# A hybrid decoder step on one core: the sample's cross attention takes its cache unsplit, and four instead of six couples of up-projection tiles are begun early

## The chip, the core and the metric

The kernel runs on one core of one Trainium2 chip. The core has five engines with instruction queues of their own: TensorE (PE; its weight loads are shown apart as PEld), VectorE (DVE), ScalarE (ACT), GpSimd (POOL) and SyncE (SP), which here issues nearly all transfers. Each queue is worked off in order, and engines wait for one another through semaphores. The metric is the device time of one launch in microseconds, lower being better. The kernel before was run three times: median 2275.94 us, 2272.01 to 2283.53.

## The reference, cut to what matters

A prompt of 1024 rows and 8 samples of 8 rows go through one layer that shares all weights. The four token mixers come first; the two parts that the change touches are the last two steps:

```python
x = _ln(ALPHA * x + mix, lp['ln1_g'], lp['ln1_b'])
qm = (x @ lp['w_mq']).reshape(n, L, X_HEADS, X_HD)
s = jnp.einsum('nqhe,nkhe->nhqk', qm, mem_k, preferred_element_type=jnp.float32) * (X_HD ** -0.5)
pr = jax.nn.softmax(s, axis=-1)
att = jnp.einsum('nhqk,nkhe->nqhe', pr.astype(mem_v.dtype), mem_v).reshape(n, L, D_MODEL) @ lp['w_mo']
x = _ln(ALPHA * x + att, lp['ln2_g'], lp['ln2_b'])
ff = jnp.square(jax.nn.relu(x @ lp['w_up'])) @ lp['w_down']
x = _ln(ALPHA * x + ff, lp['ln3_g'], lp['ln3_b'])
```

There are 4 heads of 256 and 256 memory tokens. For the samples `mem_k` and `mem_v` are caches of their own (`cache_mem_k`, `cache_mem_v`: 8 samples x 256 x 4 x 256 each, 16.8 MB together), so every sample multiplies with another matrix and has only 8 query rows for it. The feed forward is 1024 x 4096 and back.

## The kernel before, in words

All is float32. A large product is made from matmuls on float32r operands: an operand is split into `hi`, its rounded copy (made by ACT), and `lo`, the remainder (subtracted by DVE), and `hi*hi + hi*lo + lo*hi` are summed in PSUM. `split_w` (L85 to L108) does this to a 128x1024 weight tile: one 512 KB load into a `raw` buffer by SP, one cast (L100), one subtraction (L106).

**Cross attention** (`rest`, from L1589). For the prompt, sixteen steps over eight tiles of 128 rows and two head pairs `hp` make the scores: `scores` is 24 matmuls of 512 columns into `sc` (L129), then a softmax on ACT and DVE, and later four transposes (`ptr`, L1505) turn the probabilities. After each step's softmax, `next(sample)` takes some steps of the generator `sample_x`, which holds the samples' attention, so its instructions stand between those of the prompt. In `sample_x` the query rows are first made with `w_mq` (`acc`) and turned (`qtr`). A part is four samples and one head pair. For each part `own` lays out a stationary operand with zeros for other samples' queries, and each of the four samples' key tiles goes through `split_w` and eight matmuls of 256 columns with 64 stationary columns (`sps`, L1553). The same is done with the value tiles into `ops` (L1578). `spread` (L1566) multiplies each part's result with a constant `sel` to turn it (`otr`). That is 32 tiles, 32 casts, 32 subtractions and 256 matmuls of this kind. The loads take `raw` buffers from a ring of four (`wraw2` and `wraw`, two each). After the last step the folded output weights (`fold`) and `w_mo` are loaded through the two buffers of `wraw` (`out_proj`, from L1372).

**Feed forward** (`feed`, from L1664). The up projection is done by a two-by-two scheme of the Strassen kind over sixteen couples `p` of column tiles: seven products of blocks for four, on pieces of `x` called `11`, `21`, `22`, `t1` to `t4`. Class `Hat` makes the pieces from the rows turned on PE: `first` makes `11` and `21`, `second` makes `22` and `t2` tile by tile, `rest` makes `t3`, `t1` and `t4`. A product is 24 matmuls of 272 columns (L117). `begin(p)` does a couple's two products with `11` and `21` ahead of the loop, while `Hat.second` still works on the rest: couples 0 and 1 keep the results (`vr`), the others write them to DRAM (`vd`) from the pool `vs`, and `recall` brings them back inside the loop. The piece `t4` takes the memory of the pool `vs`, so it is made after the last write to `vd` has gone out. Then the loop over the couples makes the other products in the order `t2`, `t3`, `t1`, `t4`, `22`, and for a couple that was not begun early also `11` and `21`. The weight sums `s1` to `s4` that these need are made by `first_sums` on POOL (`sw`, L1779 and L1780) and by `prep` on DVE (L1792, L1794); `split` (L1686, L1687) makes the operands `wo`, up to three ahead. Each couple's results are combined on POOL (`sh`, L1925 to L1928) and written to DRAM (`hs`); `w_down` blocks are summed on DVE and written as `wt`. All of these transfers are issued by SP in the order of the code, tied by `behind` (L1695).

The order of instructions in each queue is settled when the program is built, by a scheduler that moves independent work up or down.

Of the kernel before, what the change touches and what calls it, by code (L numbers as in the profile page):

```python
# [8 lines left out]
F32 = mybir.dt.float32  # L9
F32R = mybir.dt.float32r  # L10
# [30 lines left out]

LOADS, SPLITS, TAIL, OX = 4, 2, 6, 12

EARLY_PAIRS = 6

MORE = [(0, i) for i in range(1, 8)] + [(1, 0)]
UNITS = dict(first=8, pre=1, blk=1, u1=1, chain=1, smp=1, norm=1, d0=3, d1=1, z=1)
# [2 lines left out]
class Kern:  # L50
# [1457 lines left out]
    def sample_x(self, x1, out):  # L1508

        nc, I, pm = self.nc, self.I, self.pm
        sel = pm.tile([64, 32], F32, name="sel")
        nc.sync.dma_start(sel, I["sel"])
        z = pm.tile([128, 512], F32, name="zs")
        qs = pm.tile([128, 8, 64], F32, name="qs")
        row = lambda name: pm.tile([128, 512], F32, name=name, tag="row", bufs=2)

        def own(src, name):

            t = pm.tile([128, 4, 4, 64], F32R, name=name, tag="own", bufs=2)
            nc.vector.memset(t.rearrange("p a s x -> p (a s x)").bitcast(F32), 0.0)
            t4 = t.rearrange("p (a b) s x -> p a b s x", b=2)
            for s4 in range(4):
                v, c = src(s4), 8 * s4
                nc.scalar.copy(t4[:, :, :, s4, c:c + 8], v)
                nc.vector.tensor_sub(t4[:, :, :, s4, 32 + c:40 + c], v, t4[:, :, :, s4, c:c + 8].bitcast(F32))
# [16 lines left out]
        parts = [(s2, hp) for s2 in range(2) for hp in range(2)]  # L1544
        for s2, hp in parts:
            qz = own(lambda s4: qs[:, 4 * hp:4 * hp + 4, 32 * s2 + 8 * s4:32 * s2 + 8 * s4 + 8].rearrange("p (a b) q -> p a b q", b=2), "qz")
            ps = self.wk_ps("sps", "acc")
            for s4 in range(4):
                w = self.split_w(I["cmk"][4 * s2 + s4, hp])
                for h in range(2):  # L1550
                    for ct in range(2):
                        for i in range(2):
                            nc.tensor.matmul(ps[0:64, h * 256:h * 256 + 256], qz[:, 2 * h + ct, s4, :], w[i][:, (2 * h + ct) * 256:(2 * h + ct) * 256 + 256],  # L1553
                                             start=s4 == h == ct == i == 0, stop=s4 == 3 and h == ct == i == 1)
                yield
            r, lo = slice(64 * s2 + 32 * hp, 64 * s2 + 32 * hp + 32), row("slo")
            nc.scalar.copy(lo[r], ps[32:64])
            nc.vector.tensor_add(z[r], lo[r], ps[0:32])
        pT = pm.tile([128, 4, 128], F32, name="pTs")
        nc.scalar.copy(pT, self.keys_first(self.softmax(z, "ps")))  # L1560
        pT = pT.rearrange("p (h k) (s a t) -> p k h s a t", k=2, s=2, a=2)
        def spread(s2, hp, o):

            tr = self.wk_ps("otr")[:, 0:128].rearrange("p (k t) -> p k t", t=32)
            for k in range(4):
                nc.tensor.matmul(tr[:, k, :], o[0:64, k * 128:k * 128 + 128], sel, start=True, stop=True)  # L1566
            nc.scalar.copy(out[:, 4 * hp:4 * hp + 4, 32 * s2:32 * s2 + 32], tr)

        last = None
        for s2, hp in parts:  # L1570
            pz = own(lambda s4: pT[:, :, :, s2, hp, 8 * s4:8 * s4 + 8], "pz")
            ps = self.wk_ps("ops", "acc")
            for s4 in range(4):
                w = self.split_w(I["cmv"][4 * s2 + s4, hp])
                for kb in range(2):
                    for h in range(2):
                        for i in range(2):
                            nc.tensor.matmul(ps[0:64, h * 256:h * 256 + 256], pz[:, 2 * kb + h, s4, :], w[i][:, (2 * kb + h) * 256:(2 * kb + h) * 256 + 256],  # L1578
                                             start=s4 == kb == h == i == 0, stop=s4 == 3 and kb == h == i == 1)
                if s4 == 1 and last:  # L1580
                    spread(*last)
                yield
            o = row("so")
            nc.scalar.copy(o[0:64], ps[0:64])
            last = s2, hp, o
        yield
        spread(*last)

# [75 lines left out]
    def feed(self, hat, y, s_xb, s_y, w3, w4, wb):  # L1664
# [89 lines left out]
        hat.second(y, 5, self.gp)  # L1754
        begin(1)
        hat.second(y, 6, self.gp)
        begin(2)
        hat.second(y, 7, self.gp)
        begin(3)
        begin(4)  # L1760
        begin(5)
        fetch(0)
        fetch(1)
        hat.rest("t3")
        hat.rest("t1")
        s_t4.close()
        hat.room(s_up.enter_context(self.pool("xh4", side="right")), ("t4",))
        hat.rest("t4")
        s_y.close()
        self.mmp, self.mmi = ring4 + [self.psw] * 4, -1  # L1770
        up = s_up.enter_context(self.pool("uh"))
# [34 lines left out]
        todo, ops = operands(), []  # L1806

        def nxt():
            while len(ops) < (3 if not st["wide"] else 4):
# [377 lines left out]
def _consts():  # L2187
# [31 lines left out]
    return {"sel": np.tile(np.eye(32, dtype=f), (2, 1)), "cmask": cm, "amask": am, "tmask": tm, "smask": np.tile(sm, (128, 1)), "teye": te.reshape(128, 8, 32), "ident": np.eye(128, dtype=f)}  # L2219


def _prep(a):
# [95 lines left out]
```

## Time and profile before

| what | value |
|---|---|
| median of three runs | 2275.94 us |
| the profiled execution | 2281.47 us, its span 2279.7 us |
| mean granted TensorE clock | 0.977 of full |
| PE, PEld busy | 95%, 86% |
| DVE, ACT, POOL busy | 60%, 43%, 19% |
| chain that ended last | PE 71%, DVE 10%, DMA 9%, issue 4%, ACT 3%, POOL 2% |

The busy shares are means over stages that differ, and the chain tells which work the end waited for. A matmul's duration in a row includes the time to run empty; the distance between starts is what a stream of them costs. Rows name output and inputs by the program's names, `x16` counts instructions, and what stands in brackets is the idle time of that engine before the row and what ended it.

### The profile page before, as it was taken

The page shows a single profiled execution, that of the slowest core. Times are in us where ns is not written, and L with a number is a line of the kernel's source. Part 1 is how long each engine was busy: PE and PEld are TensorE (multiplying, and loading weights), DVE is VectorE, ACT ScalarE, POOL GpSimd, SP SyncE. Part 2 cuts the span into 40 slices and gives each one's busy share as a digit, 9 for nine tenths or more (in the row PEclk, how much of TensorE's full clock was granted, in tenths as well). Part 3 has the DMA queues.
Part 4 walks back from the last instruction along what each step waited for, and adds up shares of the span by engine and source line. Part 5 has one row for each costly group of instructions (what it writes and reads, how often), then busy time and mean ns, then how long its engine had stood idle before and what let it go on. Part 6 is the DMA issues. An engine that isn't in the chain of part 4 may idle for free.

```text
span 2279.7 us, 36377 instructions
## 1 busy us (share of the span) xinstructions
PE 2175.1 (95%) x13702; PEld 1949.2 (86%) x13702; DVE 1374.5 (60%) x2748; ACT 978.7 (43%) x1888; POOL 425.7 (19%) x484
## 2 busy tenths in 40 slices
PE   8998999999999999999999999998789999999997
PEld 8987777898989888998998888778789999788886
DVE  3356767755665764343333877586667776655558
ACT  4333433145555655444231566335334444543432
POOL 0111111012311200123220500000445444100100
PEclk9998989999999999999999999999899999999999
DMA  5322333135444435555324355624487767975534
GB/s 191 103 75 61 99 90 98 38 129 186 152 132 130 130 114 171 162 173 162 102 64 149 120 190 167 221 102 141 162 292 261 248 238 239 325 240 182 178 118 171
DMA packets 186071, 359.41 MB, mean 158 GB/s; under 512 B 36312, under 2 KB 92776, under 8 KB 185896
## 3 DMA queue, kind: packets, MB, share of 16 engines
q1 hardware_dynamic: 175448, 321.52, 43.2%
q0 software_dynamic: 10448, 35.57, 4.6%
q8 instruction: 108, 1.77, 0.3%
q14 instruction: 67, 0.55, 0.1%
HBM read 252.18 MB, written 104.84 MB: 157 GB/s over the span
## 4 chain that ended last, share of the span: by engine, by line
PE 71%; DVE 10%; DMA 9%; issue 4%; ACT 3%; POOL 2%; SPq 1%; DVEq 0%; ACTq 0%; POOLq 0%
PE mm L117 21%; PE m L117 12%; PE dn L1989 11%; PE mm L129 8%; PE sc L129 3%; PE pp L117 3%; PE ds L1994 1%; DVE tpr L1013 1%; DVE wlo L106 1%; DMA vp<-in_vpages,pt 1%; ACT whi L100 1%; DMA Li<-Ld 1%; PE wtp L502 1%; DVE Ti L1014 1%; PE gr L965 1%
## 5 line engine op out<-in xcount | busy, mean ns | idle before, releaser
L117 PE MATMUL mm<-ah,whi 128*128 128x384 f32 (+1 forms) x1176 | 395.7, 336 | 8.4 <-ACT ah L277 4.9
L117 PE MATMUL mm<-al,whi 128*128 128x384 f32 (+1 forms) x1176 | 392.5, 334 | 0.6 <-DVE al L278 0.6
L117 PE MATMUL mm<-ah,wlo 128*128 128x384 f32 (+1 forms) x1176 | 391.7, 333 | 0.6 <-DVE wlo L106 0.6
L1989 PE MATMUL dn<-dop 128*128 128x512 f32 x1344 | 318.8, 391 | 3.7 <-ACT dop L1686 3.5
L1989 PEld LDWEIGHTS dn<-dop 128*128 128x128 f32 x1344 | 251.7, 188 | 60.6 <-ACT dop L1686 5.2
L106 DVE TENSOR_TENSOR wlo<-wraw,whi 128x1024 fp32r<-128x1024 f32 (+2 forms) x177 | 196.1, 1117 | 174.1 <-ACT whi L100 172.6
L100 ACT CAST whi<-wraw 128x1024 fp32r<-128x1024 f32 (+1 forms) x162 | 165.8, 1032 | 258.0 <-PE mm L117 101.6
L117 PEld LDWEIGHTS mm<-ah,whi 128*128 128x128 f32 x1176 | 224.4, 191 | 18.0 <-ACT ah L277 5.5
L117 PEld LDWEIGHTS mm<-al,whi 128*128 128x128 f32 x1176 | 224.1, 191 | 7.0 <-issue 3.5
L117 PEld LDWEIGHTS mm<-ah,wlo 128*128 128x128 f32 x1176 | 224.1, 191 | 4.3 <-issue 1.9
L1687 DVE TENSOR_TENSOR dop<-wraw,dop 128x512 fp32r<-128x512 f32 x224 | 151.3, 712 | 118.2 <-ACT dop L1686 117.6
L117 PE MATMUL m<-xht,wo 128*128 128x272 f32 x1024 | 202.7, 293 | 16.8 <-ACT wo L1686 10.5
L1686 ACT CAST dop<-wraw 128x512 fp32r<-128x512 f32 x224 | 131.2, 619 | 167.8 <-PE dn L1989 117.3
L117 PEld LDWEIGHTS m<-xht,wo 128*128 128x128 f32 x1024 | 165.8, 192 | 17.7 <-ACT wo L1686 10.7
L129 PE MATMUL mm<-wlo,ah 128*128 128x512 f32 (+1 forms) x488 | 170.1, 351 | 2.7 <-DVE wlo L106 2.7
L129 PE MATMUL mm<-whi,ah 128*128 128x512 f32 (+1 forms) x488 | 170.5, 351 | 0.8 <-ACT stA L300 0.5
L117 PE MATMUL m<-xh,wo 128*128 128x272 f32 x768 | 153.6, 293 | 6.1 <-DVE r L1901 6.1
L129 PE MATMUL mm<-whi,al 128*128 128x512 f32 (+1 forms) x448 | 156.5, 349 | 0.0
L117 PE MATMUL m<-xlt,wo 128*128 128x272 f32 x512 | 149.5, 292 | 0.0
L117 PEld LDWEIGHTS m<-xh,wo 128*128 128x128 f32 x768 | 124.7, 192 | 6.7 <-ACT wo L1686 2.6
L117 PE MATMUL m<-xl,wo 128*128 128x272 f32 x384 | 111.9, 292 | 0.0
L129 PEld LDWEIGHTS mm<-wlo,ah 128*128 128x128 f32 x488 | 93.9, 193 | 16.7 <-DVE wlo L106 3.6
(510 smaller groups left out, 4313.1 us busy)
## 6 DMA issues: line engine op xcount, KB each, us to landing
wraw<-hs SPq DMA_DIRECT2D x112, 256.0 KB
wraw<-in_w_up SPq DMA_DIRECT2D x38, 512.0 KB
wraw<-in_w_gate SPq DMA_DIRECT2D x32, 512.0 KB
dw<-in_w_down SPq DMA_DIRECT2D x32, 512.0 KB
hs<-sh SPq DMA_DIRECT2D x64, 256.0 KB
wt<-dw SPq DMA_DIRECT2D x32, 512.0 KB
wraw<-wt SPq DMA_DIRECT2D x64, 256.0 KB
wraw<-in_w_down SPq DMA_DIRECT2D x48, 256.0 KB
```

Of the source, the lines that this page charges most:

```text
L100: nc.scalar.copy(hi[:, c], raw[:, c])
L106: nc.vector.tensor_sub(lo[:, c], raw[:, c], hi[:, c].bitcast(F32))
L117: nc.tensor.matmul(ps[:, :n], a, b, start=first and i == 0, stop=last and i == len(steps) - 1, skip_group_check=not first)
L129: nc.tensor.matmul(ps[:, :n], a, b, start=i == 0, stop=i == len(steps) - 1)
L502: self.nc.tensor.transpose(ps[:b.shape[-1], j * 128:j * 128 + 128], b, self.ident)
L965: nc.tensor.matmul(g[hh][:nb, j, :nb], p[HR[hh], pr, cs], q[HR[hh], pr, cs], start=True, stop=True)
L1013: nc.vector.tensor_mul(tv, Ti[:, 0:h, 0:t + 1], Li[:, 0:t + 1, t:t + 1].rearrange("p s o -> p o s").to_broadcast([128, h, t + 1]))
L1014: nc.vector.tensor_reduce(Ti[:, 0:h, t:t + 1], tv, axis=AX.X, op=ALU.add)
L1686: nc.scalar.copy(o[:, 0], src)
L1687: nc.vector.tensor_sub(o[:, 1], src, o[:, 0].bitcast(F32))
L1989: nc.tensor.matmul(ps[j], hs[:, a, c], w[:, b], start=first and k == 0, stop=last and k == 2, skip_group_check=n >= 16 and steps[n][0] in ...
L1994: nc.tensor.matmul(sp, rows[p][:, smp[i]].rearrange("p a n -> p (a n)"), ops[n][1][:, b], start=i != 2 and p == 0 and b == 0, stop=p == 15 ...
```

## The change

Two edits are made in one step. In `sample_x`, `split_w` is gone. `products` loads two samples' tiles at a time into the same `raw` buffers (now called `kvraw`) and multiplies them as they are, in float32: eight matmuls of 256 columns for two samples, each with 32 stationary columns, and the result of head `h` and sample `s` goes to its own 32 PSUM rows (`r = 64 * h + 32 * s`). A group of eight has four such row blocks in turn, twice. There are 16 groups, so 128 matmuls. A `raw` buffer is now held until its matmuls have read it. `spread` turns the result with two transposes for a head pair, twice instead of four times four matmuls. In `feed`, couples 4 and 5 are no longer begun early; `fetch(0)` stands earlier, and couple 0's weight sums are made by DVE in place, and its operands split, before `t3`, `t1` and `t4`, instead of by `first_sums(0)` after them.

```diff
-EARLY_PAIRS = 6
+EARLY_PAIRS = 4
...
-            t = pm.tile([128, 4, 4, 64], F32R, name=name, tag="own", bufs=2)
+            t = pm.tile([128, 4, 2, 4, 32], F32, name=name, tag="own", bufs=2)
...
+        def raw(src):
+            self.wi += 1
+            t = self.raws[self.wi % len(self.raws)].tile([128, 1024], F32, name="kvraw", tag="raw")
+            nc.sync.dma_start(t, src)
+            return t
+
+        def products(ps, o, name, hp, col, first, last):
+
+            for j in range(4):
+                w = []
+                for a in range(2):
+                    w.append(raw(I[name][2 * j + a, hp]))
+                    if a:
+                        for i in range(2):
+                            for h in range(2):
+                                c, st = col(h, i)
+                                for s in range(2):
+                                    r = 64 * h + 32 * s
+                                    nc.tensor.matmul(ps[r:r + 32, o:o + 256], st[:, s, j, :], w[s][:, 256 * c:256 * c + 256],
+                                                     start=first and j == i == 0, stop=last and j == 3 and i == 1)
+                    yield
...
-            for s4 in range(4):
-                w = self.split_w(I["cmk"][4 * s2 + s4, hp])
...
-                            nc.tensor.matmul(ps[0:64, h * 256:h * 256 + 256], qz[:, 2 * h + ct, s4, :], w[i][:, (2 * h + ct) * 256:(2 * h + ct) * 256 + 256],
...
+        ps = self.wk_ps("sps", "acc")
+        for hp in range(2):
+            qz = own(lambda j: qs[:, 4 * hp:4 * hp + 4, 16 * j:16 * j + 16].rearrange("p k (s q) -> p k s q", q=8), "qz")
+            yield from products(ps, 256 * hp, "cmk", hp, lambda h, ct: (2 * h + ct, qz[:, 2 * h + ct]), hp == 0, hp == 1)
...
-                nc.tensor.matmul(tr[:, k, :], o[0:64, k * 128:k * 128 + 128], sel, start=True, stop=True)
+                nc.tensor.transpose(tr[:, 128 * k:128 * k + 128], o[:, 128 * k:128 * k + 128], self.ident)
...
         hat.second(y, 6, self.gp)
+        fetch(0)
         begin(2)
         hat.second(y, 7, self.gp)
         begin(3)
-        begin(4)
-        begin(5)
-        fetch(0)
+
+        a11, a12, a21, a22 = blocks(0)
+        x0 = hat.pool.tile([128, 512], F32, name="x0", tag="ex8", bufs=1)
+        nc.vector.tensor_sub(x0, a11, a21)
+        nc.vector.tensor_add(a21, a21, a22)
+        nc.vector.tensor_sub(a11, a21, a11)
+        nc.vector.tensor_sub(a12, a12, a11)
+        ops = [split(a11)]
+        hat.rest("t3")
+        ops.append(split(x0))
+        hat.rest("t1")
+        ops.append(split(a21))
         fetch(1)
-        hat.rest("t3")
-        hat.rest("t1")
         s_t4.close()
         hat.room(s_up.enter_context(self.pool("xh4", side="right")), ("t4",))
         hat.rest("t4")
+        ops.append(split(a22))
...
-            for p in range(16):
+            yield split(blocks(0)[1])
+            for p in range(1, 16):
...
-        first_sums(0)
```

Two places show how the queues move. On PE, in the middle of the cross attention, this stands before: one sample's matmuls, with the prompt's transposes (`ptr`) and score matmuls (`sc`) among them.

```order
L1553 MATMUL sps<-wlo,qz 64x256
L1505 MATMUL ptr<-ident,p 128x128
L1553 MATMUL sps<-whi,qz 64x256
L1505 MATMUL ptr<-ident,p 128x128 x3
L129 MATMUL sc<-whi,ah_12520 128x512
```

The same place in the change:

```order
L129 MATMUL sc<-wlo,ah_12520 128x512
L1543 MATMUL sps<-kvraw,qz 32x256 x16
L1505 MATMUL ptr<-ident,p 128x128 x4
L129 MATMUL sc<-whi,ah_12520 128x512
L129 MATMUL sc<-whi,al_12523 128x512
```

The groups now stand whole, in twelve runs of eight or sixteen matmuls (four of sixteen, eight of eight), and between most neighbouring runs stand the 24 `sc` of a step.

On DVE, where the loop over the couples begins, this stands before: the last operand of an early couple (`wo<-wraw`), the remainders of `t4` (`xlt` from `xtb` and `xt`), then couple 0's and couple 1's sums and operands.

```order
L1687 TENSOR_TENSOR wo<-wraw,wo 128x512
L2127 TENSOR_TENSOR xlt_15628<-xtb,xht_15627 128x4x128 x4
L2127 TENSOR_TENSOR xlt_15628<-xt_15118,xht_15627 128x8x16
L1792 TENSOR_TENSOR sw<-wraw 128x512
L1794 TENSOR_TENSOR sw<-wraw,sw 128x512
L1687 TENSOR_TENSOR wo<-sw,wo 128x512 x3
```

In the change, where `xlt_15166` is the remainder of `t4`:

```order
L1770 TENSOR_TENSOR wraw<-wraw 128x512
L1691 TENSOR_TENSOR wo<-x_15123,wo 128x512
L1771 TENSOR_TENSOR wraw<-wraw 128x512
L2140 TENSOR_TENSOR xlt_14765<-xta,xht_14764 128x4x128
L1691 TENSOR_TENSOR wo<-wraw,wo 128x512 x3
L2140 TENSOR_TENSOR xlt_15166<-xtb,xht_15165 128x4x128 x4
L2140 TENSOR_TENSOR xlt_15166<-xt_14772,xht_15165 128x8x16
```

Four of couple 0's operands now stand ahead of the remainders of `t4`, which on DVE are what waits for the write to `vd`.

## Rows read from the trace of the kernel before

**Rows 1.** Busy time by engine from 1346 to 1441 us, with clock and DMA share.

```profile
1346.00:1441.00 95.00, 94.99 (x575) 80.78 (x574) 71.95 (x141) 57.46 (x130) 0.00 (x0) 1.00 0.53 173
```

**Rows 2.** Chain of waits from 1310 to 1445 us, shares by line.

```profile
by line: PE sc L129 54.9%; PE sps L1553 11.7%; PE ops L1578 11.2%; PE ptr L1505 5.4%; DVE wlo L106 3.6%; DMA wraw<-in_w_mq 3.6%; PE otr L1566 3.0%; PE acc L1436 1.9%; ACT whi L100 1.5%; issue 1.0%; POOL yacc L1465 0.9%; PE mm L129 0.9%; DVE
```

**Rows 3.** Chain of waits, then timelines, where the loop over couples begins.

```profile
1573.06 18.18 PE m L117 x144
...
1595.23 2.50 DVE L2127 TENSOR_TENSOR xlt<-xtb,xht 128x512 fp32r<-128x512 f32 x4 [14.44 <-DMA vd<-vs]
...
1598.07 1.58 POOL L1779 TENSOR_TENSOR sw<-wraw 128x512 f32<-128x512 f32 x1 [45.52 <-DVE xlt L2127]
...
1601.06 1.66 ACT L1686 CAST wo<-sw 128x512 fp32r<-128x512 f32 x3 [6.45 <-POOL sw L1780]
...
1601.73 0.59 PE L117 MATMUL m<-xht,wo 128*128 128x272 f32 x1 [10.51 <-ACT wo L1686]
```

**Rows 4.** Busy time by engine around the feed forward's start, columns as in 1.

```profile
1592.00:1608.00 16.00, 6.16 (x28) 5.96 (x29) 10.01 (x14) 5.39 (x11) 6.24 (x5) 0.57 0.22 75
...
1643.00:1717.00 74.00, 67.23 (x500) 66.64 (x501) 49.41 (x88) 28.41 (x48) 35.86 (x37) 0.94 0.88 293
```

**Rows 5.** Timeline of PE: first and last of sixteen score matmuls.

```profile
1352.57 0.28 PE L1553 MATMUL sps<-whi,qz 128*64 128x256 f32 x1
...
1354.37 0.28 PE L1553 MATMUL sps<-wlo,qz 128*64 128x256 f32 x1
```

**Rows 6.** Timeline of PE: unsplit f32 matmuls and transposes, elsewhere; L696's durations.

```profile
514.84 0.59 PE L696 MATMUL dg<-dv,ws 128*128 128x256 f32 x2
...
639.34 1.07 PE L558 MATMUL ysp<-vp,wP 128*32 128x128 f32 x16
...
1407.09 1.08 PE L1566 MATMUL otr<-sel,so 64*128 64x32 f32 x8
...
1408.10 0.66 PE L1505 MATMUL ptr<-ident,p 128*128 128x128 f32 x4
...
L696 PE MATMUL dg<-dv,ws x24: 218/378/483, 514.8 to 540.4; 128*128 128x256 f32 x16, 64*64 64x64 f32 x8
```

**Rows 7.** Slices of L558 alone: passes in flight on PE (first x).

```profile
639.34:639.35 0.01, 0.01 (x2) 0.01 (x2) 1.00 0.00 0
...
639.48:639.49 0.01, 0.01 (x4) 0.01 (x2) 1.00 0.00 0
```

**Rows 8.** A weight load's issue, and the cast that waits for it.

```profile
1449.76 0.33 SPq L99 DMA_DIRECT2D wraw<-in_w_mo  x1
...
1455.95 1.05 ACT L100 CAST whi<-wraw 128x1024 fp32r<-128x1024 f32 x1 [2.97 <-DMA wraw<-in_w_mo]
```

**Rows 9.** Chain of waits from 1310 to 1445 us: twenty of the score matmuls.

```profile
1366.16 4.63 PE sc L129 x20
```

**Rows 10.** Timeline of PE where the output projection begins.

```profile
1453.03 0.73 PE L1436 MATMUL acc<-whi,ah 128*128 128x512 f32 x2 [1.59 <-ACT whi L100]
...
1454.29 0.73 PE L1436 MATMUL acc<-wlo,ah 128*128 128x512 f32 x2 [0.30 <-DVE wlo L106]
```

**Rows 11.** Timeline of DVE: first sum (L1880) of couples 0, 3 and 6.

```profile
1606.91 0.93 DVE L1880 TENSOR_TENSOR u<-vr,m 128x272 f32<-128x272 f32 x2
...
1659.52 0.44 DVE L1880 TENSOR_TENSOR u<-v,m 128x272 f32<-128x272 f32 x1 [0.22 <-PE m L117]
...
1716.93 0.42 DVE L1880 TENSOR_TENSOR u<-v,m 128x272 f32<-128x272 f32 x1
```

**Rows 12.** Timelines of POOL and PE in couple 2.

```profile
1639.72 1.26 POOL L1779 TENSOR_TENSOR sw<-wraw 128x512 f32<-128x512 f32 x1 [5.58 <-DMA wraw<-in_w_up]
...
1643.69 0.56 PE L117 MATMUL m<-xht,wo 128*128 128x272 f32 x1 [5.70 <-DVE u L1880]
```

**Rows 13.** The page's first line.

```profile
span 2279.7 us, 36377 instructions
```

More of the change, by code (lines that the diff above doesn't have):

```diff
@@ L1512, in sample_x @@
         nc, I, pm = self.nc, self.I, self.pm
-        sel = pm.tile([64, 32], F32, name="sel")
-        nc.sync.dma_start(sel, I["sel"])
-        z = pm.tile([128, 512], F32, name="zs")
         qs = pm.tile([128, 8, 64], F32, name="qs")
@@ L1519, in own @@
         def own(src, name):
-            t = pm.tile([128, 4, 4, 64], F32R, name=name, tag="own", bufs=2)
-            nc.vector.memset(t.rearrange("p a s x -> p (a s x)").bitcast(F32), 0.0)
-            t4 = t.rearrange("p (a b) s x -> p a b s x", b=2)
-            for s4 in range(4):
-                v, c = src(s4), 8 * s4
-                nc.scalar.copy(t4[:, :, :, s4, c:c + 8], v)
-                nc.vector.tensor_sub(t4[:, :, :, s4, 32 + c:40 + c], v, t4[:, :, :, s4, c:c + 8].bitcast(F32))
-            return t
+            t = pm.tile([128, 4, 2, 4, 32], F32, name=name, tag="own", bufs=2)
+            nc.vector.memset(t.rearrange("p a b s x -> p (a b s x)"), 0.0)
+            for j in range(4):
+                nc.scalar.copy(t[:, :, :, j, 8 * j:8 * j + 8], src(j))
+            return t
+        def raw(src):
[4 more added lines that the diff above has]
+        def products(ps, o, name, hp, col, first, last):
+            for j in range(4):
+                w = []
[10 more added lines that the diff above has]
+                    yield
         steps = self.sample_w(x1, "w_mq")
@@ L1542, in sample_x @@
         nc.scalar.copy(qs.rearrange("p k t -> p (k t)"), qt)
[L1544 to L1548, printed above, removed]
-                w = self.split_w(I["cmk"][4 * s2 + s4, hp])
-                for h in range(2):
-                    for ct in range(2):
-                        for i in range(2):
-                            nc.tensor.matmul(ps[0:64, h * 256:h * 256 + 256], qz[:, 2 * h + ct, s4, :], w[i][:, (2 * h + ct) * 256:(2 * h + ct) * 256 + 256],
[L1554 to L1565, printed above, removed]
-                nc.tensor.matmul(tr[:, k, :], o[0:64, k * 128:k * 128 + 128], sel, start=True, stop=True)
-            nc.scalar.copy(out[:, 4 * hp:4 * hp + 4, 32 * s2:32 * s2 + 32], tr)
+        ps = self.wk_ps("sps", "acc")
@@ new lines, in sample_x, with spread @@
+        for hp in range(2):
+            qz = own(lambda j: qs[:, 4 * hp:4 * hp + 4, 16 * j:16 * j + 16].rearrange("p k (s q) -> p k s q", q=8), "qz")
+            yield from products(ps, 256 * hp, "cmk", hp, lambda h, ct: (2 * h + ct, qz[:, 2 * h + ct]), hp == 0, hp == 1)
+        pT = pm.tile([128, 4, 128], F32, name="pTs")
+        nc.scalar.copy(pT, self.keys_first(self.softmax(ps, "ps")))
+        pT = pT.rearrange("p k (g j q) -> p k g j q", j=4, q=8)
+        def spread(hp, o):
+            tr = self.wk_ps("otr")
+            for k in range(2):
+                nc.tensor.transpose(tr[:, 128 * k:128 * k + 128], o[:, 128 * k:128 * k + 128], self.ident)
+            for k in range(2):
+                for h in range(2):
+                    nc.scalar.copy(out[:, 4 * hp + 2 * h + k, :].rearrange("p (j s q) -> p s j q", s=2, q=8),
+                                   tr[:, 128 * k + 64 * h:128 * k + 64 * h + 64].rearrange("p (s j q) -> p s j q", s=2, q=8))
@@ L1569, in sample_x @@
         last = None
-        for s2, hp in parts:
-            pz = own(lambda s4: pT[:, :, :, s2, hp, 8 * s4:8 * s4 + 8], "pz")
+        for hp in range(2):
+            pz = own(lambda j: pT[:, 2 * hp:2 * hp + 2, :, j, :].rearrange("p k (h s) q -> p (k h) s q", s=2), "pz")
             ps = self.wk_ps("ops", "acc")
[L1573 to L1580, printed above, removed]
+            for i, _ in enumerate(products(ps, 0, "cmv", hp, lambda h, kb: (2 * kb + h, pz[:, 2 * kb + h]), True, True)):
+                if i == 2 and last:
@@ L1583, in sample_x @@
             o = row("so")
-            nc.scalar.copy(o[0:64], ps[0:64])
-            last = s2, hp, o
+            nc.scalar.copy(o[:, 0:256], ps[:, 0:256])
+            last = hp, o
         yield
@@ L1804, in operands @@
                     yield split(raw[n][:, o:o + 512], "dop")
-        todo, ops = operands(), []
+        todo = operands()
         def nxt():
@@ L2218, in _consts @@
     sm = np.concatenate([np.arange(256) % 64 != 0, np.arange(64) % 8 != 0]).astype(f)
-    return {"sel": np.tile(np.eye(32, dtype=f), (2, 1)), "cmask": cm, "amask": am, "tmask": tm, "smask": np.tile(sm, (128, 1)), "teye": te.reshape(128, 8, 32), "ident": np.eye(128, dtype=f)}
+    return {"cmask": cm, "amask": am, "tmask": tm, "smask": np.tile(sm, (128, 1)), "teye": te.reshape(128, 8, 32), "ident": np.eye(128, dtype=f)}
 def _prep(a):
```

## The prediction

> **What bounds the kernel now.** I read the two stretches that the change touches, not the means. For the cross attention, first the busy times of its stretch, then the chain of waits. Between 1346 and 1441 us PE is busy for 94.99 of 95 us at full clock, while DVE has 23 and ACT 38 us left and the DMA engines are used to 0.53 [rows 1]. The chain is PE nearly throughout: `sps` 11.7%, `ops` 11.2% and `otr` 3.0% of the 135 us from 1310 to 1445 [rows 2]. So only PE time counts there. The casts and subtractions that go (32 of each) lie beside it and I cost them at nothing: the cover is PE's own work, 95 us against 72 busy on DVE, and with less work on both sides that relation stays.
>
> For the feed forward I read the stretch where the loop begins. The chain shows PE without a break for 18.18 us (144 matmuls: the early couples 3, 4, 5) up to 1591.24. Then DVE waits until 1595.23 for the writes to `vd`, its remainders of `t4` follow, POOL waits for these until 1598.07, ACT for POOL's sums until 1601.06, and PE starts couple 0 only at 1601.73, after 10.51 us [rows 3]. From 1592 to 1608 the granted clock is 0.57 on the mean, so part of couple 0 ran at the lower level, 1.2 GHz [rows 4]. Inside the loop, later, the DMA engines are used to 0.88 at 293 GB/s from 1643 to 1717 [rows 4].
>
> **Cross attention, the price of the new matmuls.** The old `sps` and `ops`: 22.9% of 135 us is 30.9 us, which fits 256 at 0.12 us (sixteen starts spread over 1.80 us [rows 5]). The new ones have no row here, so bounds come from unsplit matmuls elsewhere. One such matmul leaves two records, two passes. With 256 columns and 128 stationary ones, two passes take 0.59 us in all and one 0.378, so the second starts 0.21 us after the first [rows 6]: a pass holds its columns of the array for 0.212 us. The nearest row to the new form is L558: 32 stationary columns, outputs at 32-row blocks, two blocks in turn, 128 columns. There 16 passes take 1.07 us together [rows 6], and two are in flight at once from the start, four 0.13 us later [rows 7]. So passes for different row blocks start in pairs, one pair per at most 0.134 us (1.07 / 8), where transposes of 128 columns, which cannot overlap, need (0.66 - 0.27) / 3 = 0.13 us each [rows 6]. Two blocks do overlap. The change has four in turn. If four overlap, 128 matmuls are 256 passes or 64 rounds of 0.212 us = 13.6 us (at most 64 x 0.268 = 17.1, from L558 doubled). If only two overlap, 128 rounds, 27.1 us. If none, 54.3 us. I take four: the blocks write disjoint rows, and nothing in L558 shows the second block costing the first any time. For each of the twelve runs I add 0.18 us, an estimate for running empty on both sides. That makes 15.8 us.
>
> The Trainium skill, "TensorE: Matmul & The Clock Gate", section "Measured speedup vs the span model", gives 2.38 times for three column tiles, so less than the count; by that, 79% of the ideal, the rounds would be an estimated 17.2 us and the whole forecast 3.6 us higher. The pair in L558 shows no such loss, and no run here has three or four.
>
> The turning: `otr` 3.0% is 4.05 us now, four times eight passes of 1.08 us [rows 6]; then four transposes of 0.13 and two changes of form, 0.7 us. So PE saves 30.9 + 4.05 - 15.8 - 0.7 = 18.5 us.
>
> **What is late next.** The old code freed a `raw` buffer after the subtraction, the new one after the matmuls, two pairs deep. A weight load with its neighbours took 6.2 us from issue to the cast that waited for it [rows 8]. A pair is refilled while PE does the 24 `sc` of a step (5.6 us; twenty took 4.63 [rows 9]) and a transposition group (0.66 us), so it comes about when it is needed: I allow 2.5 us over the stage, with 0 and 12 (1 us for each run) as ends. At the start of the output projection PE waited 1.59 and 0.30 us for the split of `w_mo` [rows 10]; in the change 62 instead of 37 matmuls stand ahead of that, and I count these 1.9 us as gained. `fold` loads then wait for the last value tiles, but four output tiles' matmuls with its first piece (24 x 4.63 / 20 = 5.6 us) cover them. Sum for this stage: 18.5 + 1.9 - 2.5 = **17.9 us**.
>
> **Feed forward.** Couples 4 and 5 take 48 matmuls each, 18.18 / 3 = 6.06 us [rows 3]; both leave the part before the loop and come back inside it, 12.1 us moved, nothing removed. A product of 24 matmuls is then 3.03 us; an early couple has five (15.15), a full one seven (21.2).
> - The gap: with the operands of `t2`, `t3`, `t1` split ahead of `t4`, PE after couple 3 waits for ACT alone, which has a relu, a square and two casts in line, 0.55 us each (three casts take 1.66 [rows 3]): an estimate of 2.5 us. On DVE the last of these operands is done by about then, since it loses couples 4 and 5's four subtractions. `t4` still waits for the write to `vd` (1595.23 - 1591.24 = 4.0 us after PE's end) and takes 2.8 us more, 6.8; PE reaches it after 2.5 + two products, 8.6 us. Hidden, by 1.8 us. POOL, which then starts with couple 1, has a whole couple for it.
> - The clock: couple 0's first sum came 5.18 us after its start (1601.73 to 1606.91 [rows 3, 11]) where 3.03 suffice: 2.1 us gained if the shorter gap leaves the clock up.
> - Couples 0 to 3: 1606.91 to 1659.52, 52.6 us [rows 11] for 45.5 of matmuls. Of the 7.1 of waiting, 5.70 is one wait in couple 2, behind POOL and a load of `w_up` [rows 12], which SP issues behind couple 0's results. Its order does not change, so the wait stays.
> - Couples 3 to 6: 57.4 us now for 48.5 of matmuls. A full couple moves 5.05 MB (results 1.9, `w_up`, `w_down`, `wt` 1.05 each), an early one with `recall` 5.6 MB, which at 293 GB/s [rows 4] are 17.2 and 19.1 us: above 15.15, below 21.2. So the waits here are bandwidth, and the moved matmuls fill them: 60.6 us of matmuls, 1 us of waits left, 61.6.
>
> From 1573.06 to couple 6's first sum it is 143.9 us now. Then: 6.06 + 2.5 + 3.03 + 52.6 + 61.6 = 125.8. Gain **18.1 us**. Ends: 8 us if half is given back, 24 if couple 2's wait goes too.
>
> **Sum.** 36.0 us. The profiled execution took 2281.47 us (span 2279.7 [rows 13]), 0.24% above the median; 2281.5 - 36.0 = 2245.5 for it, 2275.9 - 36.0 = 2240 against the median.
>
> **Rivals.**
> - *Two blocks overlap, not four* (17%). For: only two were ever seen. Then 27.1 + 2.2 + 0.7 against 34.95: 4.9 saved, the loads come in time, 6.8 with the boundary; with 18.1: 2251.
> - *The feed forward gives half* (15%): DVE stands in order, and its sums for couple 0 wait for `fetch(0)`, or the loop gives the gap back in couple 2. 9 instead of 18: 2249. Together with the first, 3%: 2260.
> - *No overlap at all* (7%), because accumulation into one bank goes in order: 54.3 + 2.2 + 0.7 = 57.2, 22.2 lost, 1.9 gained at the boundary: 2278, no change. Against it: L558. The change breaks even at a pass of 0.20 us counted singly.
> - *Slower: the cache loads come late* (4%). Place: the ring of two pairs, now held until PE has read it. For: SP must wait for PE, and PE's step gets shorter. Price: 16 pairs, each late by what 6.2 us exceed the matmuls between; it decides at (36 + 2.5) / 16 = 2.4 us for each. If nothing overlapped beyond one run, 4 us for each: 2276 - 38.5 + 64 = 2301. Against it: 0.53 of DMA share now.
> - *More than forecast* (4%): couple 2's wait shrinks and no load is late: 2225 or below.
>
> **How the numbers follow.** My forecast has 50%, by its own terms 2231 to 2248. For 8 in 10 the range must take in the two middle rivals: 2224 to 2261. About 0.5% (11 us) is what a measurement of this kernel can tell from no change; below 2264.5 lie the forecast, the first two rivals, both together and the last: 0.89. Same 0.07, slower 0.04.
>
> **What would show it.** `sps` and `ops` passes: rounds of four starting together, a run of eight in about 1.0 us (two rounds at once: 1.9; singly: 3.6), and PE busy without gaps ahead of each run; a gap there, ended by `kvraw`, is the late load. At the start of the loop a gap of PE of 2 to 3 us instead of 10.5 with the clock at 1.00, and no wait of `xlt` passed on to PE. In couple 2 still a wait near 6 us; from couple 3 on none over 1 us. Wrong would be the forecast if runs last 1.9 us, if PE's gap after couple 3 ends on DVE or `w_up`, or if waits in couples 3 to 6 persist.

## The result and the profile after

| | median us | range | ratio to before, 95% interval |
|---|---|---|---|
| before, same chip | 2273.98 | 2269.54 to 2283.53 | |
| changed | 2246.0 | 2244.94 to 2257.71 | 0.9892 (0.987 to 0.9915) |
| changed, run again beside other runs of the kernel before | 2245.25 | 2243.58 to 2247.74 | 0.9879 (0.9857 to 0.99) |

The forecast was 2240 us, 36 us less than before. The ratio 0.9892 is 24.6 us of 2276, the second one 27.5. The sign and the range held, the gain came out short.

The two profiled spans differ by more, 36.5 us, and part of that lies ahead of the change. The chain of waits passes four transposes of the last rows (L1477) just before the cross attention begins; up to there both kernels do the same work. The first line of the page of the changed kernel:

```profile
span 2243.2 us, 36135 instructions
```

That row of its chain (start, duration):

```profile
1306.31 0.46 PE tr L1477 x4
```

And the same row of the kernel before:

```profile
1311.41 0.46 PE tr L1477 x4
```

Ahead of the mark there are 5.1 us of difference in work that the edit left alone. Most of it goes with the granted clock. One stretch of it, 300 to 350 us, by the busy times of the kernel before (the third column from the end is the clock):

```profile
300.00:350.00 50.00, 48.15 (x359) 39.69 (x357) 25.92 (x93) 17.66 (x47) 6.83 (x10) 0.80 0.22 56
```

The same stretch of the changed kernel, where 0.06 x 50 = 3 us less are lost to the clock (another such stretch is 850 to 900 us, 0.93 against 0.97):

```profile
300.00:350.00 50.00, 47.88 (x374) 40.00 (x373) 27.92 (x99) 17.76 (x47) 6.83 (x10) 0.86 0.24 63
```

So two executions are better compared by the rest of the span behind this mark: 2279.7 - 1311.41 = 968.3 before, 2243.2 - 1306.31 = 936.9 after, 31.4 less. The experiments use it too. In four profiles of equal PE work (the change, its repetition and the two with another order of row blocks) the rest is 936.9, 939.4, 938.7 and 939.4, while in all kernels the mark itself lies anywhere from 1298.2 to 1313.5.

**The cross attention after.** Busy times of its stretch, as in [rows 1]:

```profile
1341.00:1419.00 78.00, 78.00 (x549) 55.91 (x548) 27.45 (x68) 21.36 (x75) 0.00 (x0) 1.00 0.56 196
```

PE's timeline, with the first run of eight matmuls, one of the four runs of sixteen, and the wait in the output projection, as in [rows 10]:

```profile
1341.21 1.07 PE L1543 MATMUL sps<-kvraw,qz 128*32 128x256 f32 x16
...
1392.61 1.93 PE L1543 MATMUL ops<-kvraw,pz 128*32 128x256 f32 x32
...
1442.37 0.73 PE L1436 MATMUL acc<-whi,ah 128*128 128x512 f32 x2 [0.85 <-ACT whi L100]
```

PE is busy without a gap, for 78.0 us where it was 95. Eight matmuls (sixteen records) take 1.07 us with the way out, and by the chain 1.00 us until the next matmul starts. The two waits at the output projection, 1.59 and 0.30 [rows 10], became one of 0.85. By the slices of L1543, as in [rows 7], the first run has four passes in flight from its start and eight 0.24 us later, when the next four have started and the first four are on their way out:

```profile
1341.22:1341.23 0.01, 0.01 (x4) 0.01 (x4) 1.00 0.00 0
...
1341.46:1341.47 0.01, 0.01 (x8) 0.01 (x4) 1.00 0.00 0
```

**The feed forward after.** The end of the early couples in the chain:

```profile
1550.41 6.07 PE m L117 x48
```

Timelines of PE, where couple 0 starts and where it comes to `t4`, and of DVE, the first sums (L1893) of couples 0, 3 and 6, as in [rows 11]:

```profile
1558.53 0.39 PE L117 MATMUL m<-xht,wo 128*128 128x272 f32 x1 [2.06 <-ACT wo L1690]
...
1565.28 0.39 PE L117 MATMUL m<-xlt,wo 128*128 128x272 f32 x1 [0.15 <-DVE xlt L2140]
...
1565.75 0.77 DVE L1893 TENSOR_TENSOR u<-vr,m 128x272 f32<-128x272 f32 x2
...
1615.23 0.44 DVE L1893 TENSOR_TENSOR u<-v,m 128x272 f32<-128x272 f32 x1 [0.22 <-PE m L117]
...
1681.10 0.42 DVE L1893 TENSOR_TENSOR u<-v,m 128x272 f32<-128x272 f32 x1
```

Busy times of couple 0's first two products, of the stretch behind couple 2's wait, and of couples 3 to 6:

```profile
1558.50:1566.00 7.50, 7.32 (x55) 7.10 (x56) 7.49 (x10) 3.40 (x7) 3.99 (x3) 1.00 0.40 147
...
1598.00:1615.20 17.20, 16.64 (x110) 16.67 (x111) 11.56 (x21) 5.57 (x10) 7.08 (x8) 0.81 0.85 262
...
1615.20:1681.10 65.90, 61.85 (x489) 61.44 (x488) 46.84 (x72) 29.34 (x53) 36.00 (x35) 1.00 0.77 261
```

The gap of 10.51 us is one of 2.06, ended by ACT; `t4` stops PE for 0.15, and the clock is at its upper level in couple 0. From couple 3's first sum to couple 6's it is 65.87 us, with PE busy for 61.85. What PE waited for inside the loop (us in total, times, longest):

```profile
PE m L117 <- DVE u L1893: 8.6, 2, 6.0
...
PE m L117 <- DVE r L1914: 1.5, 1, 1.5
```

The 6.02 us stand in couple 2, as before [rows 12]. The queue of SP, then DVE's timeline there, then PE:

```profile
1582.51 0.33 SPq L1699 DMA_DIRECT2D hs<-sh  x1
...
1586.94 0.90 SPq L1699 DMA_DIRECT2D wraw<-in_w_up  x2
...
1594.65 1.76 DVE L1805 TENSOR_TENSOR sw<-wraw 128x512 f32<-128x512 f32 x1 [4.66 <-DMA wraw<-in_w_up]
...
1597.99 0.77 DVE L1893 TENSOR_TENSOR u<-v,m 128x272 f32<-128x272 f32 x2
...
1598.57 0.57 PE L117 MATMUL m<-xht,wo 128*128 128x272 f32 x1 [6.02 <-DVE u L1893]
```

SP stands until 1582.51, when POOL has finished `sh`, issues couple 0's results and only at 1586.94 the loads of `w_up`. DVE, which has to make couple 3's sum (L1805) first by its order, waits for the load until 1594.65; couple 2's first sum (L1893) stands behind it, and PE behind that. The granted clock is 0.81 on the mean in the 17.2 us that follow, which by my estimate costs another 0.19 x 17.2 = 3.3 us.

The 1.49 us are in couple 3, the 2.56 us in couple 4. For the latter, timelines of POOL, DVE and PE:

```profile
1641.24 1.26 POOL L1793 TENSOR_TENSOR sw<-sw,wraw 128x512 f32<-128x512 f32 x1
...
1642.54 0.69 DVE L1807 TENSOR_TENSOR sw<-wraw,sw 128x512 f32<-128x512 f32 x1 [4.70 <-POOL sw L1793]
...
1643.63 0.39 PE L117 MATMUL m<-xht,wo 128*128 128x272 f32 x1 [2.56 <-DVE u L1893]
```

Here the load had come, but POOL, in order, had couple 3's `sh` (from 1633.95) ahead of the second sum for couple 5, and DVE stood 4.70 us for it. In the repetition of this kernel the waits in couples 3 and 4 are 1.28, 2.45 and 1.21 us.

### The profile page after: what moved, and what is told of

Its sections match the earlier page's. It is cut to its first block, busy times and chain, and to the rows that moved or that the text cites. A ratio compares the mean times of both kernels' runs of the same rounds, so it can differ in the third digit from the quotient of the medians.

```text
span 2243.2 us, 36135 instructions
## 1 busy us (share of the span) xinstructions
PE 2148.9 (96%) x13674; PEld 1916.8 (85%) x13674; DVE 1338.9 (60%) x2678; ACT 942.6 (42%) x1838; POOL 428.0 (19%) x482
## 3 DMA queue, kind: packets, MB, share of 16 engines
q8 instruction: 107, 1.75, 0.3%
## 4 chain that ended last, share of the span: by engine, by line
PE 69%; DMA 11%; DVE 11%; ACT 4%; issue 3%; POOL 2%; SPq 1%; DVEq 0%; ACTq 0%; POOLq 0%
PE mm L117 20%; PE m L117 13%; PE dn L2002 11%; PE mm L129 8%; PE sc L129 3%; PE pp L117 2%; DMA add<-gate 1%; PE ds L2007 1%; DVE tpr L1013 1%; DMA wraw<-in_w_gate 1%; ACT whi L100 1%; DVE wlo L106 1%; PE gr L965 1%; DMA Li<-Ld 1%; PE wtp L502 1%
## 5 line engine op out<-in xcount | busy, mean ns | idle before, releaser
L106 DVE TENSOR_TENSOR wlo<-wraw,whi 128x1024 fp32r<-128x1024 f32 (+2 forms) x145 | 158.6, 1100 | 173.8 <-ACT whi L100 173.4
L100 ACT CAST whi<-wraw 128x1024 fp32r<-128x1024 f32 (+1 forms) x130 | 132.9, 1027 | 229.7 <-PE mm L117 100.9
```

The lines of the kernel that those rows point to most:

```text
L100: nc.scalar.copy(hi[:, c], raw[:, c])
L106: nc.vector.tensor_sub(lo[:, c], raw[:, c], hi[:, c].bitcast(F32))
```

## The experiments

All ratios are to the kernel before on the same chip. "Rest" is the span less the start of the mark, each from one profile, so that differences of 2.5 us or less say little.

| kernel | median us | ratio, interval | span - mark = rest |
|---|---|---|---|
| cross attention alone (ca_only) | 2257.58 | 0.9925 (0.9896 to 0.9953) | 2256.0 - 1305.64 = 950.4 |
| feed forward alone (feed_only) | 2259.84 | 0.9935 (0.9912 to 0.9957) | 2259.1 - 1305.01 = 954.1 |
| changed again (after_again) | 2245.25 | 0.9879 (0.9857 to 0.99) | 2241.8 - 1302.44 = 939.4 |
| two blocks in turn (two_blocks) | 2243.5 | 0.9853 (0.9819 to 0.9886) | 2246.6 - 1307.89 = 938.7 |
| block after block (one_block) | 2240.45 | 0.9854 (0.9823 to 0.9886) | 2237.6 - 1298.16 = 939.4 |
| twelve groups to two blocks (two_rows) | 2257.17, one run | | 2255.4 - 1307.47 = 947.9 |
| twelve groups to one block (one_row) | 2275.59, one run | | 2273.8 - 1303.52 = 970.3 |
| four early, sums late (four_late_prep) | 2252.31 | 0.9894 (0.9857 to 0.993) | 2254.3 - 1304.94 = 949.4 |
| six early, sums early (six_early_prep) | 2246.31 | 0.9878 (0.9851 to 0.9906) | 2251.1 - 1308.43 = 942.7 |
| stores behind loads (fetch_first) | 2229.64 | 0.9805 (0.9776 to 0.9834) | 2236.0 - 1307.12 = 928.9 |
| and reading back later (recall_last) | 2233.13 | 0.9814 (0.9792 to 0.9837) | 2238.1 - 1313.46 = 924.6 |

**The two edits apart.** The first kernel is the one before with the hunks of `sample_x` alone, the second the one before with the rest of the diff, which begins:

```diff
-EARLY_PAIRS = 6
+EARLY_PAIRS = 4
```

> The cross attention's edit alone; feed forward as before, six early couples. My theory: the two edits are independent, and this one is worth what lies between the profiles of before and after from the first score matmuls to the first couple's start, 17.5 us (17.9 forecast): a ratio near 0.992, and in the trace the same runs of 1.00 us for eight matmuls and no wait for kvraw, and the loop's gap of 10.5 us as before. Rival: the edits only pay together, because the gain is lost in the feed forward's DMA-bound couples or in a lower clock: a ratio of 0.996 or above.

> The feed forward's edit alone; cross attention as before. My theory: worth 14.1 us (35.83 to couple 6's first sum, less 5.1 that lay ahead of the cross attention and 17.5 of that stage, and 0.9 in couple 7), a ratio near 0.994, with a gap of 2.1 us before couple 0 and the waits of 6.0 in couple 2 and about 4 in couples 3 and 4. Rival: the forecast's 18.1 is right and the 4 us in couples 3 and 4 are an accident of that run: ratio 0.992, and no waits over 1 us in couples 3 and 4.

Alone, the cross attention gives 968.3 - 950.4 = 17.9 us of rest and the feed forward 14.2; the ratios 0.9925 and 0.9935 say 17 and 15 with some 5 or 6 to either side. Together that would be 0.986. For the whole change, run again:

> The changed kernel once more, beside the next two on one chip. The two parts alone measured 0.9925 and 0.9935, together 0.986 if they add up; the kernel with another order of row blocks, which PE works off in the same time, 0.9853 and 0.9854; the changed kernel itself 0.9892 with an interval up to 0.9915. Additive: 0.984 to 0.988, 2240 to 2246. If the two edits take something from each other: 0.989 or above.

It gave 0.9879, the upper end of the additive case, and 0.9892 at first: near the sum, and whether a few us get lost between the edits these runs can't tell. Where couple 0 starts, PE's timeline of the first and of the second:

```profile
1577.20 0.60 PE L117 MATMUL m<-xht,wo 128*128 128x272 f32 x1 [10.51 <-ACT wo L1690]
```

```profile
1573.77 0.40 PE L117 MATMUL m<-xht,wo 128*128 128x272 f32 x1 [2.06 <-ACT wo L1686]
```

So the gap belongs to the second edit alone.

**Which row blocks overlap.** Two orders of the same eight matmuls, `h, i, s` (two blocks in turn) and `h, s, i` (block after block):

```diff
-for i in range(2):
-    for h in range(2):
+for h in range(2):
+    for i in range(2):
...
-for i in range(2):
-    for h in range(2):
-        c, st = col(h, i)
-        for s in range(2):
+for h in range(2):
+    for s in range(2):
+        for i in range(2):
+            c, st = col(h, i)
```

> The changed kernel with another order of the eight matmuls of a group: head 0's four first (two row blocks in turn), then head 1's. Theory 1, passes start in the order of the stream, and one for a busy block holds up all behind it: only two overlap, eight rounds of 0.212 instead of four, a run of eight matmuls takes 1.85 instead of 1.00 us, sixteen groups add 13.6 us: about 2260. Theory 2, each row block has a queue of its own that is deep enough for a group: still 1.00 us and 2246.

> The changed kernel with the two matmuls of a row block next to each other, block after block. Theory 1, in the order of the stream: a block's four passes go one after the other and the next block's first pass starts with the last of them, 13 rounds, 2.9 us a run of eight, sixteen groups add 30 us: about 2276, the same as before the change. Theory 2, a queue for each block: 1.00 us and 2246. In between, a short queue for each block: 1.4 to 2.4 us.

Theory 2 held. PE's timeline, one run of each, and then the slices at the start of the second's first run:

```profile
1342.21 1.08 PE L1543 MATMUL sps<-kvraw,qz 128*32 128x256 f32 x16
```

```profile
1346.07 1.09 PE L1543 MATMUL sps<-kvraw,qz 128*32 128x256 f32 x16
```

```profile
1332.87:1332.88 0.01, 0.01 (x3) 0.01 (x4) 1.00 0.00 0
...
1332.91:1332.92 0.01, 0.01 (x4) 0.01 (x8) 1.00 0.00 0
...
1333.15:1333.16 0.01, 0.01 (x8) 0.01 (x4) 1.00 0.00 0
```

Even with all four passes of a block next to each other in the program, four are in flight within 0.04 us of the start and the run is as short. One rival is that the scheduler, which moves independent work, had put the blocks back in turn. The trace speaks against it: the first passes of the four blocks start 13, 13 and 14 ns apart here (1332.846 to 1332.886 us), 7, 20 and 7 ns with two blocks in turn, and 7 ns each in the change, which is about 6.7 ns for every place in the order written (2, 2 and 2 places, 1, 3 and 1, and 1 each). So matmuls are handed out in the order of the program, but one whose row block is busy does not hold up those behind it for other blocks. That each queue is worked off in order, as said at the start, does not hold on PE across row blocks, at least over a group of eight. The Trainium skill, "TensorE: Matmul & The Clock Gate", section "The mechanism", has matmuls start and end strictly in the order of the program; by that the run would have 13 rounds, an estimated 2.9 us. The trace doesn't agree: 1.09 us.

The counter-test takes the blocks away:

```diff
-r = 64 * h + 32 * s
+r = 64 * h + 32 * s if j == 3 else 32 * s
...
-start=first and j == i == 0, stop=last and j == 3 and i == 1
+start=True, stop=True
```

This is the kernel with two blocks; the one with one block has `else 0` in place of `else 32 * s`.

> Left out: in twelve of the sixteen groups all eight matmuls write to row blocks 0 and 32 alone, each over the one before it, so the attention is not summed; the work of PE is the same in number and shape. The other four groups use all four blocks. The theory of a queue for each row block, with a pass that holds its block for 0.212 us: these twelve groups have eight passes for each of two blocks, 1.85 us a run of eight instead of 1.07, and the other four stay at 1.07; the stage is 12 x 0.85 = 10 us longer. Rival, that the short run comes from the 32 stationary columns and not from the blocks: 1.07 throughout.

> Left out: as in the run with two row blocks, but the twelve groups write to block 0 alone. Queue for each block: sixteen passes in line, 16 x 0.212 = 3.4 us, 3.55 a run, the stage 12 x 2.5 = 30 us longer, near 2276. Rival, 32 columns are fast by themselves: 1.07.

PE's timelines, a run of the twelve groups:

```profile
1342.02 1.92 PE L1543 MATMUL sps<-kvraw,qz 128*32 128x256 f32 x16
```

```profile
1337.90 3.64 PE L1543 MATMUL sps<-kvraw,qz 128*32 128x256 f32 x16
...
1358.56 1.07 PE L1543 MATMUL sps<-kvraw,qz 128*32 128x256 f32 x16
```

1.92 and 3.64 against 1.07: each step is (3.64 - 1.92) / 8 = 0.215 us for a pass, where the forecast took 0.212, and the rest grew by 9.3 and 31.7 us over 938.6, the mean of the four equal ones. So the price of a pass and the overlap were as forecast, and a run of four blocks is 3.4 times as fast as one of one block. The groups that kept all four blocks in the same kernel stayed at 1.07, so it is the blocks and not the 32 columns or the overwriting.

**The two halves of the feed forward's edit.** The first is the kernel with the cross attention alone and these lines, the second the changed kernel with the same lines the other way round, six for four:

```diff
-EARLY_PAIRS = 6
+EARLY_PAIRS = 4
...
-        begin(4)
-        begin(5)
```

> The new cross attention, with four early couples, but couple 0's sums and operands made as before, by POOL behind the remainders of t4. My theory: the two edits of the feed forward act in different places. The gap stays near 10.5 us with the lower clock behind it, and the moved products gain only what couples 3 to 6 give, 12.1 + 57.4 - 65.9 = 3.6 us: about 2254 where the cross attention's edit alone gave 2257.6. Rival, the forecast's terms: 7.9 us there, 2250; rival, the gap depends on the number of early couples too, and is shorter by some us.

> The changed kernel with six early couples again; couple 0's sums and operands early, as in the change. My theory: the early operands close the gap by themselves (near 2 us instead of 10.5, since t4 waits for its writes while two products run), and the number of early couples is worth only 2 to 4 us in couples 3 to 6: 2246 to 2250. Rival: with six, the last write to vd ends later against the two products, t4 is late by some us, and the gap comes back in couple 0: 2252 or more.

PE's timelines at the start of couple 0, of the first and of the second:

```profile
1564.95 0.60 PE L117 MATMUL m<-xht,wo 128*128 128x272 f32 x1 [10.46 <-ACT wo L1690]
```

```profile
1570.60 0.29 PE L117 MATMUL m<-xht,wo 128*128 128x272 f32 x1
...
1579.28 0.39 PE L117 MATMUL m<-xlt,wo 128*128 128x272 f32 x1 [1.97 <-DVE xlt L2142]
```

With four couples and late sums the gap is the old one, and the rest is 1.0 us shorter than with the cross attention alone (3.6 expected). With six and early sums there is no gap at all, and `t4` is 1.97 us late, the rival's mechanism at a small size; the rest is 7.7 us shorter. Both together: 950.4 - 938.6 = 11.8. The early operands carry most of this edit; having four instead of six adds 1 to 4 us by the rest. The timed runs don't settle that second number: 0.9894 against 0.9925 would be 7 us, near the rival's 7.9, with intervals that overlap, and 0.9878 against 0.9879 would be nothing.

**What the loop still waited for.** One move, for the wait in couple 2:

```diff
-            if p:
-                store(p - 1)
             if 1 <= p < EARLY_PAIRS - 1:
                 recall(p + 1)
...
                     bring(2 * (p - 14) + n)
+            if p:
+                store(p - 1)
```

> The changed kernel with one move: the results of the couple before are stored behind the loads of w_up, not ahead of them. My theory: couple 2's wait of 6.0 us is DVE standing at couple 3's sum for a load of w_up that SP issues behind stores that wait for POOL; with the load issued about 6 us earlier the wait falls below 1 us, and couples 3 and 4 (1.5 and 2.6) keep theirs, since they hang on the order of POOL: 2240 to 2242. Rival: the later stores keep POOL's buffers, its sums come later, and the wait moves to the next couple: 2245 to 2249.

The theory held for couple 2, and the move was worth more than forecast: the rest is 928.9, 9.7 us less than 938.6. SP's queue, then the first sums of couples 3 and 6, SP again, and the one wait of PE left in the loop from couple 1 on:

```profile
1568.82 7.78 SPq L1699 DMA_DIRECT2D wraw<-in_w_up  x2
...
1576.65 1.29 SPq L1699 DMA_DIRECT2D hs<-vr  x1
...
1611.12 0.43 DVE L1893 TENSOR_TENSOR u<-v,m 128x272 f32<-128x272 f32 x1
...
1673.21 0.42 DVE L1893 TENSOR_TENSOR u<-v,m 128x272 f32<-128x272 f32 x1
...
1597.07 0.33 SPq L1699 DMA_DIRECT2D v<-vd  x1
...
1597.93 1.75 SPq L1699 DMA_DIRECT2D wraw<-in_w_up  x2
...
1611.70 0.37 PE L117 MATMUL m<-xht,wo 128*128 128x272 f32 x1 [3.56 <-ACT u L1719]
```

The loads are now issued by 1576.6 and couple 2's wait is gone, as are those of couples 3 and 4, which I had expected to stay. I take it that with earlier loads POOL has its sums made in time; no run shows that by itself. A wait of 3.56 us is new in couple 3: SP stands until 1597.07 at the reading back of `v`, the loads of `w_up` behind it are issued at 1597.93, POOL's sums wait for these until 1606.12, ACT's operands for the sums, and couple 3's first sum on DVE for the operands. Couples 3 to 6 take 1673.21 - 1611.12 = 62.1 us.

The next step moves that reading back behind the loads as well. In the first kernel for it the list of operands asked whether a couple was begun before that couple had been read back, so that from couple 2 on the products took other operands than they should; its 2228.7 us count for nothing:

> The kernel with the results stored behind the loads of w_up, and the reading back of couples 2 and 3 moved behind these loads too. In the run before, PE still waited 3.6 us in couple 3: SP stood at the reading of v, which has one buffer, and issued the loads of w_up 6 us after those of w_down. Theory: that wait goes, 3 to 4 us less, and nothing else: 3.6 below the kernel before it, a ratio near 0.979. Rival: v comes back too late for couple 3's first sum, and the wait has another name: no gain.

With the list in order:

```diff
-            if p not in begun:
+            if p >= EARLY_PAIRS:
...
-            if 1 <= p < EARLY_PAIRS - 1:
-                recall(p + 1)
...
                     bring(2 * (p - 14) + n)
+            if 1 <= p < EARLY_PAIRS - 1:
+                recall(p + 1)
             if p:
                 store(p - 1)
```

> As in the run before: reading back moved behind the loads of w_up, and whether a couple was begun early now asked by its number, so that its operands come in the order of its products. In the run before, that order was off, which made couples 2 and 3 multiply with other operands, so that its time told nothing. Theory: the 3.6 us that PE waited in couple 3 with the stores moved alone go, 2226, ratio near 0.979. Rival: v comes back too late for couple 3's first sum, or POOL's sums are late in another place: no gain, 0.9805.

DVE's first sums of couples 3 and 6, the one wait of PE left in the loop from couple 1 on (us in total, times, longest), and the busy times of couples 3 to 6:

```profile
1614.56 0.78 DVE L1893 TENSOR_TENSOR u<-v,m 128x272 f32<-128x272 f32 x2
...
1675.29 0.42 DVE L1893 TENSOR_TENSOR u<-v,m 128x272 f32<-128x272 f32 x1
```

```profile
PE m L117 <- DVE u L1893: 1.3, 1, 1.3
```

```profile
1614.60:1675.30 60.70, 60.16 (x477) 60.19 (x478) 45.22 (x70) 28.13 (x51) 34.18 (x33) 1.00 0.79 267
```

Couple 3's wait is 1.3 instead of 3.56 us, and the rest is 924.6, 4.3 us less than with the stores moved alone, by one profile of each. The timed runs don't show this: 0.9814 against 0.9805, with intervals wider than the difference looked for. Both are faster than the change (0.9892 and 0.9879, intervals apart). Six early couples with this order of SP weren't tried.

## Why the prediction was right, and where it was short

- **Cross attention, PE alone decides.** Right: the stage is without a gap on PE before and after, and the casts and subtractions that went were worth nothing by themselves. Forecast 17.9, measured 17.9 as rest of the kernel with this edit alone. That they agree to a tenth is luck: the terms below erred both ways, and the rest of equal kernels scatters by 2.5 us.
- **Four row blocks overlap, 15.8 us.** Right: the chain's shares by line from 1300 to 1425 us, as in [rows 2], give `sps` and `ops` 12.4% of 125, 15.5 us:

```profile
by line: PE sc L129 62.1%; PE ptr L1505 6.2%; PE sps L1543 6.2%; PE ops L1543 6.2%; DMA wraw<-fold 4.8%; DMA wraw<-in_w_mq 3.8%; PE acc L1436 2.8%; DVE wlo L106 2.8%; POOL yacc L1465 1.5%; issue 1.1%; DVE al L1481 1.0%; ACT whi L100 0.8%; P
```

  The 0.18 us for each run, for which the forecast names no row, are 0.24 here: 1.00 - 4 x 0.215 = 0.14 in the run and 0.10 ahead of it (next point). The inference from two blocks in L558 to four was the largest bet of the forecast (two rivals, at 17% and 7%), and the counter-tests bear it out. The Trainium skill, "TensorE: Matmul & The Clock Gate", section "Measured speedup vs the span model", has 2.38 times for three column tiles, 79% of the count. Here four against one are 3.64 / 1.07 = 3.4 times, 85%, with the way out of each run in it. No run had three.
- **The other terms of the stage.** 2.5 us for late cache loads were too many: no run waited. Of the 1.9 us of waiting at the output projection about 0.8 were gained: 1.59 and 0.30 became 0.85, since PE now waits for the cast of a later piece of `w_mo`, which itself waited 2.91 us for its load, and a wait of 0.25 for ACT (at 1421.93) is new. PE's stage shrank by 17.0 us by busy time where the terms gave 18.5. Most of that 1.5 stands ahead of the runs: a score matmul followed by a run keeps PE 0.33 us (in PE's timeline 1417.12 to 1417.45) where score matmuls otherwise start 0.23 apart [rows 9], some 1.1 us for the twelve runs, while the old 64-column matmuls followed after 0.23 (1437.72 to 1437.95). The errors cancelled.
- **The gap.** Right in place and cause: 2.06 against 2.5 forecast, ended by ACT, with `t4` hidden but for 0.15, and the clock at full in couple 0. From the end of the early couples to couple 3's first sum 58.1 us were forecast (2.5 + 3.03 + 52.6), and it is 1615.23 - (1550.41 + 6.07) = 58.7. Two of these terms were off by themselves: couple 0's first sum came 7.2 us after the couple's start and not 3.03, since DVE makes it behind the remainders of `t4`, and from there to couple 3's it was 49.5 us and not 52.6. PE did not wait for that sum.
- **Couple 2's wait stays.** Right, and so was the cause named for it: 6.02 us, gone when only the order in SP's queue changes.
- **The step that failed**, inside a sum whose range held, is "so the waits here are bandwidth, and the moved matmuls fill them: ... 1 us of waits left, 61.6", for couples 3 to 6. Measured: 65.87, with waits of PE of 1.49 and 2.56 us, at a DMA share of 0.77 where it was 0.88 [rows 4]. These 4.3 us over the forecast are about the whole shortfall of the feed forward (14.2 against 18.1), and waits that persist there are what the prediction itself had named as a sign of being wrong. I had divided bytes by the rate that a busy stretch showed and taken the quotient for the limit. What PE waited for in the changed kernel was order: DVE behind POOL, POOL behind its own `sh`, SP behind stores. With the kernel's transfers in another order the same stretch takes 1675.29 - 1614.56 = 60.7 us at a share of 0.79, the 60.6 of matmuls that I had worked out. The trace of the kernel before could have told me: PE's three waits in couples 3 to 6 there (1.75, 2.39 and 1.95 us) all end on DVE's `r`, and each leads back to a second sum of POOL (L1780) that stood behind `sh`. What PE waited for (us in total, times, longest), and DVE's timeline for the second of them:

```profile
PE m L117 <- DVE r L1901: 6.1, 3, 2.4
```

```profile
1686.80 0.69 DVE L1794 TENSOR_TENSOR sw<-wraw,sw 128x512 f32<-128x512 f32 x1 [3.80 <-POOL sw L1780]
```

  The load that POOL needed had come by 1681.44 us, when DVE began a sum of its own with it (L1792), and POOL, after `sh`, began only at 1684.11. So order had a part in these waits at 0.88 too; what faster transfers would have given there, no run shows.
- **The sum.** 17.9 + 14.2 = 32.1 where 36.0 were forecast, 31.4 in the pair of profiles, 29.7 with the mean of the four equal ones (938.6). The timed ratios say 25 to 28 with intervals of 5 us to either side, and 33 for the two kernels with another order of row blocks.

## What to carry to other kernels

A stretch in which the DMA engines are mostly busy (0.77 to 0.88 here) and PE waits is not thereby bound by bandwidth: follow each wait to its releaser and look at what the releaser's queue held ahead of it. When work is taken out of such a stretch or put into it, count the waits one by one and ask of each whether its queue changes. And before two profiles are compared, set a mark behind the last work that both share: here 5.1 of 36.5 us lay ahead of it.

## What was not expected of the hardware

The order of small-column matmuls in the program made no difference: with row blocks in turn (1.07 us), in pairs (1.08) or block after block (1.09) PE ran four blocks at once, two when only two were addressed (1.92), one when only one was (3.64). And moving each couple's eight stores behind two loads in one queue gave 9.7 us of rest (0.9805 against 0.9879 in the timed runs), more than half of the 17.9 that the whole rewriting of the cross attention gave.
